# Turning values and keys by 64x64 products with the identity, head by head, in place of 128x128 transposes, in a two-layer hybrid decoder

## The chip, the cores and the metric

The kernel runs on one core of a Trainium2 chip. The time is the device time of one execution in microseconds (us), median of several runs. A profile of one execution gives each engine's instructions in order of time: TensorE (PE; its weight loads PEld), VectorE (DVE), ScalarE (ACT), GpSimd (POOL) and SyncE (SP).

## What is computed

Two layers, each of four sub-layers with a residual around each, on 512 tokens of width 1024 (batch 1), all in float32. The change lies in the second one, the mixer:

```python
h = h + 0.5 * swiglu_ffn(rmsnorm(h), ffn1_w_in, ffn1_w_out)
p = rmsnorm(h) @ w_mix_in                # conv | HGRN2 (6 heads of 64) | RWKV-7 (6 heads of 64)
y = concat(short_conv(p_conv), hgrn2(p_hg), rwkv7(p_rw))
h = h + y @ w_mix_out
h = h + memory_cross_attention(rmsnorm(h), rmsnorm(mem), wq, wkv, wo)
h = h + 0.5 * swiglu_ffn(rmsnorm(h), ffn2_w_in, ffn2_w_out)

# hgrn2, chunks of 64 tokens, a state of 64x64 for each head; b is the running sum of log_f in the chunk
o     = (qc * exp(b)) @ state + att @ vc
state = exp(b_last)[..., None] * state + (kc * exp(b_last - b)).T @ vc
# rwkv7, for each token
sa    = state @ a_t
state = state * w_t + outer(sa, b_t) + outer(v_t, k_t)
y_t   = state @ r_t
```

Both recurrences are done in the kernel by chunks of 64 tokens (8 chunks). A sum over the tokens of a chunk needs a factor with the tokens on the partitions. The projections leave channels on the partitions and tokens on the columns, so some tiles have to be turned, chunk by chunk and head by head: the RWKV values `v`, the HGRN values `v`, and the HGRN keys with their decay, `kh`.

## The kernel before, in words

All activations lie as tiles of 128 channels x 512 tokens (`s` in the profile; 2 heads of 64 channels in each). A projection (`mm3`, `group_steps`) multiplies a weight tile of 128x128 by such a tile three times in a rounded 32-bit format: rounded weight by rounded input, rounded weight by the input's rest, and the weight's rest by the rounded input. So each weight block of 128x1024 that SyncE loads into `wst` (2 buffers) is rounded by ScalarE into `whi` (3 buffers) and its rest is taken by VectorE into `wlo` (3 buffers) (`load_w`, lines 461 to 470). `split` (line 603) does the same with a result: ScalarE copies it rounded, VectorE subtracts. Results stand in PSUM: projections in `pb` (3 banks), small products in `pm` (3 banks, `small()`), the RWKV chain in `pt` (2 banks).

In the mixer (`mix`, line 1308) the projections are a queue (`Fill`): 28 of the input, then keys (`mem_kv`: four heads, two weights for each in one bank, 256 columns) and values (two matrices, each in two banks) of the memory for the cross-attention, then the first output projections `out(d, 5, 8)` with the HGRN part, and after everything else `out(d, 0, 5)`. Beside it stand generators: `rw_inputs` for three pairs of RWKV heads, `rw_solve`, `rw_chain` (8 steps, one for a chunk) and `rw_post` (the group norm: two rounds of sums over heads, a scale of the three tiles by ScalarE, low-rank products) one after the other, and `hg_pair` for three pairs of HGRN heads. Their products go between those of the queue. When is decided at build time: `Clock` estimates each instruction's time, a generator says with `Need(...)` which tiles, how many free buffers (`room`) and how many free `pm` banks (`banks=[(smalls, 2)]`) its next piece wants, and `Fill.run` (line 569) takes the piece that is ready by that estimate, or else one more projection product. TensorE's instructions stand in the order in which they were written so; those of ScalarE, VectorE and SyncE are sorted by the estimated start (`issue_in_order`, line 312). On the chip each engine keeps that order.

`turned` (line 794) is called nine times in a layer: three times by `rw_inputs`, into UV (tokens of one chunk and one head; the head `j` on the half of the partitions that `1 - j` names), and six times by `hg_pair` through `tok`, for `v` and `kh`. It makes eight transposes of 128 columns (both heads and two chunks in one) into two `pm` banks, one product of 64x64 for the first chunk of the head that the transposes, which start at each chunk, leave out, and takes out what is needed in five ScalarE copies. `half(j)` are 64 partitions, `cols(c)` the 64 columns of a chunk, `c8` splits the columns by chunks.

Of the kernel before, what the change touches and what calls it, by code (L numbers as in the profile page):

```python
# [18 lines left out]
P = 128  # L19
# [8 lines left out]
C = 64  # L28
H = C // 2
NC_ = T // C  # L30
# [299 lines left out]
def trunk(ctx: ExitStack, tc: tile.TileContext, a, out, parts=("ffn1", "mix", "xa", "ffn2"), dbg=None):  # L330
    nc = tc.nc
    clock = Clock()
    ve, se, gp = (Timed(clock, e, n) for e, n in ((nc.vector, "DVE"), (nc.scalar, "ACT"), (nc.gpsimd, "POOL")))
# [16 lines left out]
    te = Pe()  # L350
# [13 lines left out]
    smalls = Banks(clock, psml, [P, T], "pm", 3)  # L364
    serials = Banks(clock, pser, [P, T], "pt", 2)
    wst, whi, wlo = (Banks(clock, wpool, [P, 1024], n, k) for n, k in (("wst", 2), ("whi", 3), ("wlo", 3)))
    big, small, serial = bigs.get, smalls.get, serials.get
# [37 lines left out]
    ident = cst[:, C_ID:C_ID + P]  # L405
# [351 lines left out]
    def c8(x):  # L757
        return x.rearrange("p (c t) -> p c t", t=C)
# [32 lines left out]
            return x.rearrange("p (c n u t) -> p c n u t", c=NC_, u=2, t=hl)[:, :, :, 1, :]  # L791
        ve.copy_predicated(v(dst), m.bitcast(I32), v(src))

    def turned(x, low, dst):


        high = 1 - low
        hs = slice(high * C, high * C + C)
        for hf in range(2):
            ps = small()  # L800
            for w in range(4):
                c = 4 * hf + w
                if c < NC_ - 1:
                    te.transpose(ps[:, w * P:(w + 1) * P], x[:, c * C:c * C + P], ident)
                else:
                    te.transpose(ps[0:C, w * P:(w + 1) * P], x[:, c * C:], ident)
                    te.matmul(ps[C:P, w * P + high * C:w * P + high * C + C], x[hs, 0:C], ident[hs, hs],
                              start=True, stop=True)
            pv = ps.rearrange("p (c j e) -> p c j e", j=2, e=C)
            se.copy(dst(low, 4 * hf, 4 * hf + 4), pv[0:C, :, low, :])  # L810
            nw = 3 + (hf == 0)
            se.copy(dst(high, 4 * hf + 1, 4 * hf + 1 + nw), pv[C:P, 0:nw, high, :])
            if hf:
                se.copy(dst(high, 0, 1), pv[C:P, 3:4, high, :])

    def evac(n, ps):
        t = sl.get()
# [3 lines left out]
    def head_sum(src):  # L821
        ps = small()
        te.matmul(ps, blk, src, start=True, stop=True)
        return ps
# [10 lines left out]
    def rw_inputs(l, n, st, p):  # L835
        UV, Z, lr, X = st["UV"], st["Z"], st["lr"], st["X"]
# [5 lines left out]
        ps = small()  # L842
# [3 lines left out]
        ps = small()  # L846
# [18 lines left out]
        ps = head_sum(t0)  # L865
# [14 lines left out]
        for hf in range(2):  # L880
# [7 lines left out]
            e = c8(G[:, tt])  # L888
# [8 lines left out]
        sl.put(lw, ag, kk, G)  # L897
        yield Need(keys=[(l, f"v{p}")])
        v = X[f"v{p}"]
        yield Need(v, banks=[(smalls, 2)])  # L900

        turned(v, 1, lambda j, c0, c1: UV[C - j * C:P - j * C, c0:c1, 2 * p + j, :])
        yield Need(room=5, spare=False)
        MSa, MSr = [sl.get() for _ in range(2)], [sl.get() for _ in range(2)]
        for hf in range(2):
# [21 lines left out]
        for hf in range(2):  # L927
            bkh = BKH[hf]
            yield Need(bkh, banks=[(smalls, 1)])
            ps = small()  # L930
# [17 lines left out]
        ps = small()  # L948
        for c in range(NC_):
            for j in range(2):  # L950
                te.matmul(ps[half(j), cols(c)], MSa[j][half(1 - j), cols(c)], UV[half(1 - j), c, 2 * p + j, :],
                          start=True, stop=True)
        se.activation(Z[:, :, p, :], c8(ps), AF.Copy)
        ps = head_sum(t0)
# [6 lines left out]
    def half(j):  # L961
        return slice(j * C, j * C + C)

    def cols(c, w=C):
        return slice(c * w, (c + 1) * w)
# [220 lines left out]
    def hg_pair(l, st, p, ys):  # L1186
        yield Need(keys=[(l, f"hg{p}")], room=11 if p else 7)
        q, k, v, g, b, kh, dec = yield from hg_gates(l, st, p)


        def tok(x):
            y = sl.get()
            turned(x, 0, lambda j, c0, c1: c8(y)[j * C:j * C + C, c0:c1, :])
            return y

        yield Need(v, banks=[(smalls, 2)], room=4)
        vT = tok(v)
        sl.put(v)

# [39 lines left out]
        w = scaled(LEVELS[0])  # L1239
        yield Need(k, q, banks=[(smalls, 1)])  # L1240
        scores(k, q, 6)
        yield Need(kh, banks=[(smalls, 2)], room=2)
        khT = tok(kh)
        sl.put(kh)
        for i, hl in enumerate(LEVELS):
# [4 lines left out]
            w = w2  # L1250
            if i == 1:

                yield Need(khT, vT, banks=[(smalls, 1)], room=1)
                ps = small()
# [17 lines left out]
        ps = small()  # L1272
# [10 lines left out]
        ps = head_sum(t)  # L1283
# [418 lines left out]
```

## Time and profile before

| | |
|---|---|
| median of 3 runs | 2441.75 us (2440.54 to 2447.37) |
| the profiled execution | 2447.83 us, its span 2446.0 us |
| TensorE busy in the span | 2398.0 us (98%) |
| VectorE busy | 1389.6 us (57%) |
| ScalarE busy | 995.7 us (41%), 94.9 of it 74 table loads |

The span is cut out of the profiled execution; what lies around it is 1.8 us. Idle time of an engine is written in square brackets behind an instruction, with the instruction that ended it; in grouped rows it stands last. A table load is ScalarE's change of function tables, an instruction of its own (ACT_TABLE_LOAD). Unrounded products (all `pm` and `pt` products) are recorded twice each, transposes and rounded products once. In a row over several instructions the second number is the time from the start of the first to the end of the last; neighbours in a pipeline overlap.

### The profile page before, as it was taken

To read this page: it belongs to the slowest core of one execution; us is meant where nothing else is said; L and a number is where in the kernel's file an instruction comes from. 1 tells how busy PE (TensorE), PEld (TensorE's weight loads), DVE (VectorE), ACT (ScalarE), POOL (GpSimd) and SP (SyncE) were. 2 spreads that over 40 slices of the span, in tenths; PEclk is the share of its full clock that TensorE was granted. 3 is DMA by queue.
4 is the path that set the end of the run, shared out by engine and by line. 5 is a ranking of instruction groups with operands and counts; after the bars stand their busy time and mean duration, and the time that the engine had idled before them with its cause. 6 is when DMAs were issued, how large, how long until landed. Compare 5 with 4: busy or idle time off the path is not lost. (4 is left out here: it accounts for less than half of the span.)

```text
span 2446.0 us, 33922 instructions
## 1 busy us (share of the span) xinstructions
PE 2398.0 (98%) x13812; PEld 1971.5 (81%) x13812; DVE 1389.6 (57%) x2172; ACT 995.7 (41%) x1416; POOL 20.8 (1%) x22
## 2 busy tenths in 40 slices
PE   7999999999999999999999999999999999999997
PEld 6888887787878888888888888877887788888886
DVE  5444456798866654444544444567987756434444
ACT  4222235756654432222332222466475534323222
POOL 0000000000000000000000000000000000000000
PEclk9999999999999999999999999999999999999998
DMA  5333333243422233333323333423333313232332
GB/s 166 95 95 94 99 109 103 82 150 122 134 84 80 65 103 97 102 93 97 95 95 100 98 95 95 132 82 121 121 117 118 96 48 100 92 98 94 96 99 74
DMA packets 94315, 246.84 MB, mean 101 GB/s; under 512 B 22096, under 2 KB 24784, under 8 KB 94160
## 3 DMA queue, kind: packets, MB, share of 16 engines
q1 hardware_dynamic: 90848, 238.56, 31.6%
q10 hardware_dynamic: 3312, 6.12, 0.7%
q8 instruction: 109, 1.79, 0.3%
q14 instruction: 46, 0.38, 0.1%
HBM read 230.48 MB, written 14.16 MB: 100 GB/s over the span
## 5 line engine op out<-in xcount | busy, mean ns | idle before, releaser
L340 PE MATMUL pb<-s,whi 128*128 128x512 f32 (+1 forms) x6160 | 1897.6, 390 | 24.3 <-ACT whi L285 16.7
L340 PEld LDWEIGHTS pb<-s,whi 128*128 128x128 f32 x6160 | 1150.2, 189 | 268.1 <-ACT whi L285 20.6
L340 PE MATMUL pb<-s,wlo 128*128 128x512 f32 (+1 forms) x3080 | 1193.5, 388 | 5.6 <-DVE wlo L285 5.6
L285 ACT ACTIVATE whi<-wst 128x1024 fp32r<-128x1024 f32 (+5 forms) x445 | 434.2, 976 | 1033.9 <-PE pb L340 637.6
L340 PEld LDWEIGHTS pb<-s,wlo 128*128 128x128 f32 x3080 | 582.9, 189 | 123.9 <-DVE wlo L285 7.7
L285 DVE TENSOR_TENSOR wlo<-wst,whi 128x1024 fp32r<-128x1024 f32 (+5 forms) x445 | 498.4, 1121 | 134.8 <-ACT whi L285 127.1
L285 DVE TENSOR_TENSOR s<-pb,s 128x512 f32<-128x512 f32 (+1 forms) x345 | 236.0, 689 | 465.0 <-PE pb L340 443.4
L285 ACT ACTIVATE s<-s 128x512 f32<-128x512 f32 (+2 forms) x458 | 282.7, 626 | 246.8 <-DVE s L285 241.2
L285 DVE TENSOR_TENSOR s<-s,s 128x512 f32<-128x512 f32 (+3 forms) x526 | 317.0, 621 | 97.0 <-ACT s L285 92.1
L285 DVE SCALAR_TENSOR_TENSOR s<-pb,s 128x512 f32<-128x512 f32 x96 | 66.4, 692 | 234.5 <-PE pb L340 234.5
L285 ACT ACT_TABLE_LOAD x74 | 94.9, 1283 | 2.9 <-PEq L1690 1.7
L285 DVE SCALAR_TENSOR_TENSOR s<-s,vec,s 128x512 fp32r<-128x512 f32 (+2 forms) x100 | 74.3, 748 | 3.8 <-ACT s L285 2.9
L340 PEld LDWEIGHTS pm<-s,s 64*64 64x64 f32 (+2 forms) x1104 | 60.4, 158 | 10.0 <-issue 4.3
L340 PE MATMUL pm<-s,s 64*64 64x64 f32 (+2 forms) x1104 | 66.7, 248 | 1.7 <-DVE s L285 0.9
L285 ACT ACTIVATE s<-s,vec 128x512 fp32r<-128x512 f32 (+1 forms) x90 | 64.3, 718 | 3.3 <-DMA s<-xT 1.7
L340 PE MATMUL pb<-whi,s 128*128 128x512 f32 x128 | 49.5, 427 | 3.3 <-DVE s L285 3.3
L340 PEld LDWEIGHTS pm<-s 64*64 64x64 f32 (+1 forms) x1152 | 33.8, 132 | 4.7 <-issue 3.2
L340 PE MATMUL pm<-s 64*64 64x32 f32 (+1 forms) x1152 | 36.3, 216 | 0.0
L285 POOL TENSOR_TENSOR rms<-rms,mhalf 128x4 f32<-128x4 f32 (+1 forms) x10 | 17.1, 1714 | 2120.7 <-DVE rms L285 2120.7
L340 PEld LDWEIGHTS pb<-whi,s 128*128 128x128 f32 x128 | 24.1, 188 | 10.8 <-DVE s L285 4.1
L285 DVE TENSOR_TENSOR s<-s 128x256 f32<-128x256 f32 (+1 forms) x79 | 31.7, 439 | 0.2
L285 ACT ACTIVATE s<-pb 128x512 fp32r<-128x512 f32 x32 | 19.0, 594 | 29.5 <-PE pb L340 29.2
(106 smaller groups left out, 741.1 us busy)
## 6 DMA issues: line engine op xcount, KB each, us to landing
wst<-ffn_w_in SPq DMA_DIRECT2D x175, 512.0 KB, 3.4
wst<-w_mix_in SPq DMA_DIRECT2D x58, 512.0 KB, 3.6
wst<-ffn_w_out SPq DMA_DIRECT2D x64, 448.0 KB, 3.3
wst<-ffn_w_out SPq DMA_DIRECT2D x32, 512.0 KB, 3.5
wst<-xattn_wk SPq DMA_DIRECT2D x16, 512.0 KB, 4.4
wst<-xattn_wv SPq DMA_DIRECT2D x16, 512.0 KB, 3.7
wst<-xattn_wq SPq DMA_DIRECT2D x16, 512.0 KB, 3.5
wst<-xattn_wo SPq DMA_DIRECT2D x32, 256.0 KB, 2.6
```

Of the source, the lines that this page charges most:

```text
L285: ins = fn(*args, **kw)
L340: self.pin(nc.tensor.matmul(*args, **kw))
```

## The change

`turned` no longer transposes. It makes 16 products of 64x64, one for each chunk and head: the 64 channels of a head and the 64 tokens of a chunk are the stationary side, the matching 64x64 corner of the identity the moving one. All go into one `pm` bank, in the place where they are wanted, and the bank is returned. `tok` copies it out whole, `rw_inputs` in two halves of the partitions. The three places that asked for two free `pm` banks ask for one.

```diff
@@ -791,27 +791,14 @@
             return x.rearrange("p (c n u t) -> p c n u t", c=NC_, u=2, t=hl)[:, :, :, 1, :]
         ve.copy_predicated(v(dst), m.bitcast(I32), v(src))
 
-    def turned(x, low, dst):
-
-
-        high = 1 - low
-        hs = slice(high * C, high * C + C)
-        for hf in range(2):
-            ps = small()
-            for w in range(4):
-                c = 4 * hf + w
-                if c < NC_ - 1:
-                    te.transpose(ps[:, w * P:(w + 1) * P], x[:, c * C:c * C + P], ident)
-                else:
-                    te.transpose(ps[0:C, w * P:(w + 1) * P], x[:, c * C:], ident)
-                    te.matmul(ps[C:P, w * P + high * C:w * P + high * C + C], x[hs, 0:C], ident[hs, hs],
-                              start=True, stop=True)
-            pv = ps.rearrange("p (c j e) -> p c j e", j=2, e=C)
-            se.copy(dst(low, 4 * hf, 4 * hf + 4), pv[0:C, :, low, :])
-            nw = 3 + (hf == 0)
-            se.copy(dst(high, 4 * hf + 1, 4 * hf + 1 + nw), pv[C:P, 0:nw, high, :])
-            if hf:
-                se.copy(dst(high, 0, 1), pv[C:P, 3:4, high, :])
+    def turned(x, low):
+
+
+        ps = small()
+        for c in range(NC_):
+            for j in range(2):
+                te.matmul(ps[half(j ^ low), cols(c)], x[half(j), cols(c)], ident[half(j), half(j)], start=True, stop=True)
+        return ps
 
     def evac(n, ps):
         t = sl.get()
@@ -897,9 +884,11 @@
         sl.put(lw, ag, kk, G)
         yield Need(keys=[(l, f"v{p}")])
         v = X[f"v{p}"]
-        yield Need(v, banks=[(smalls, 2)])
-
-        turned(v, 1, lambda j, c0, c1: UV[C - j * C:P - j * C, c0:c1, 2 * p + j, :])
+        yield Need(v, banks=[(smalls, 1)])
+
+        ps = turned(v, 1)
+        for j in range(2):
+            se.copy(UV[half(1 - j), :, 2 * p + j, :], c8(ps)[half(1 - j)])
         yield Need(room=5, spare=False)
         MSa, MSr = [sl.get() for _ in range(2)], [sl.get() for _ in range(2)]
         for hf in range(2):
@@ -1190,10 +1179,10 @@
 
         def tok(x):
             y = sl.get()
-            turned(x, 0, lambda j, c0, c1: c8(y)[j * C:j * C + C, c0:c1, :])
+            se.copy(y, turned(x, 0))
             return y
 
-        yield Need(v, banks=[(smalls, 2)], room=4)
+        yield Need(v, banks=[(smalls, 1)], room=4)
         vT = tok(v)
         sl.put(v)
 
@@ -1239,7 +1228,7 @@
         w = scaled(LEVELS[0])
         yield Need(k, q, banks=[(smalls, 1)])
         scores(k, q, 6)
-        yield Need(kh, banks=[(smalls, 2)], room=2)
+        yield Need(kh, banks=[(smalls, 1)], room=2)
         khT = tok(kh)
         sl.put(kh)
         for i, hl in enumerate(LEVELS):
```

Because the planner sees other products, other copies and other needs, it writes the mixer in another order. Three places follow, each first as it stands before and then as it stands in the changed kernel. Names are out<-in, `s_309_4722` is one tile with its number.

**ScalarE, at the keys of head 1 in the first layer.** The last row of each piece is the rounding of the second weight of that head. Before:

```order
L285 ACT_TABLE_LOAD
L285 ACTIVATE s_309_4722<-s_309_4722 128x512
L285 ACTIVATE s_308_4721<-s_307_4720 128x512
L285 ACTIVATE s_306_4719<-s_306_4719 128x512
L285 ACT_TABLE_LOAD
L285 ACTIVATE s_309_4722<-s_309_4722 128x512
L285 ACTIVATE s_306_4719<-s_306_4719 128x512
L285 ACT_TABLE_LOAD
L285 ACTIVATE s_311_4763<-s_311_4763 128x512
L285 ACTIVATE s_311_4763<-s_311_4763,oml 128x512
L285 ACTIVATE whi<-wst 128x1024
```

After:

```order
L285 ACT_TABLE_LOAD
L285 ACTIVATE s_300_4703<-s_300_4703 128x512
L285 ACTIVATE s_300_4703<-s_300_4703,oml 128x512
L285 ACTIVATE s_301_4717<-s_297_4613 128x512
L285 ACT_TABLE_LOAD
L285 ACTIVATE s_299_4698<-pm,eps_c 128x512
L285 ACT_TABLE_LOAD
L285 ACTIVATE s_299_4698<-s_299_4698 128x512
L285 ACTIVATE s_313_4776<-s_313_4776 128x512
L285 ACTIVATE s_303_4743<-s_298_4696 128x512
L285 ACTIVATE s_312_4775<-s_311_4774 128x512
L285 ACTIVATE whi<-wst 128x1024
```

The rounding of the head's first weight stands 20 rows above the last row in the piece of before, and 13 above it in that of after; five table loads stand between the two before, three after.

**VectorE, at the first value matrix.** `s_351_5621<-pb` (before) and `s_357_5761<-pb` (after) are the rests of the first bank of the first value matrix, the row behind with `<-pb` that of its second bank; `s_...<-s_...` over 256 elements are HGRN score weights. Before:

```order
L285 TENSOR_TENSOR wlo<-wst,whi 128x1024
L285 COPY_PREDICATED s_333_5170<-cst,pm 128x32x8
L285 TENSOR_TENSOR s_349_5605<-s_322_4955 128x128x2 x2
L285 TENSOR_TENSOR s_351_5621<-pb,s_350_5620 128x512
L285 TENSOR_TENSOR s_349_5605<-s_321_4951,s_349_5605 128x128x2
L285 TENSOR_TENSOR s_349_5605<-s_302_4711,s_349_5605 128x128x2
L285 TENSOR_TENSOR wlo<-wst,whi 128x1024
L285 TENSOR_TENSOR s_353_5625<-pb,s_352_5624 128x512
L285 COPY UV<-pt 64x3x64
```

After:

```order
L285 TENSOR_TENSOR s_355_5715<-s_327_5042 128x256 x2
L285 COPY UV<-pt 64x3x64
L285 TENSOR_TENSOR s_355_5715<-s_321_4957,s_355_5715 128x256
L285 TENSOR_TENSOR s_355_5715<-s_306_4765,s_355_5715 128x256
L285 TENSOR_TENSOR wlo<-wst,whi 128x1024 x2
L285 TENSOR_TENSOR s_357_5761<-pb,s_356_5760 128x512
L285 TENSOR_TENSOR s_359_5765<-pb,s_358_5764 128x512
L285 COPY_PREDICATED s_338_5337<-cst,pm 128x128x2
L285 TENSOR_TENSOR s_360_5791<-s_306_4765,s_360_5791 128x512
L285 SCALAR_TENSOR_TENSOR rwS<-rwS,pc_2833,pt 128x64
```

The two rests stand next to each other now. From the rest of key head 1's second weight to the first of them there are 105 instructions of VectorE before (the former included, the latter not) and 122 after.

**ScalarE, at the end of the mixer.** The two rows `s_...<-pb` round the two banks of the second value matrix; rows with `gneps_c` belong to the group norm's variance, rows with `vec` to its scales, `whi` rows of 384 columns to the weights of `out(d, 5, 8)`. Before:

```order
L285 ACTIVATE s_375_5994<-pb 128x512
L285 ACTIVATE s_377_5998<-pb 128x512
L285 ACTIVATE whi<-wst 128x384
L285 ACTIVATE UV<-pt 64x3x64
L285 ACTIVATE whi<-wst 128x384
L285 ACTIVATE Z<-pt 128x192
L285 ACTIVATE whi<-wst 128x384
L285 ACTIVATE s_384_6057<-s_383_6053 128x512
L285 ACTIVATE s_386_6063<-s_385_6059 128x512
L285 ACTIVATE s_388_6069<-s_387_6065 128x512
L285 ACT_TABLE_LOAD
L285 ACTIVATE s_384_6057<-pm,gneps_c 128x512
```

After:

```order
L285 ACT_TABLE_LOAD
L285 ACTIVATE s_380_6025<-s_380_6025 128x512
L285 ACTIVATE s_382_6031<-s_382_6031 128x512
L285 ACTIVATE s_379_6021<-s_379_6021,vec 128x512
L285 ACTIVATE s_381_6027<-s_381_6027,vec 128x512
L285 ACTIVATE s_384_6037<-s_384_6037 128x512
L285 DMA lr<-lowrank 128x768
L285 ACTIVATE whi<-wst 128x384
L285 ACTIVATE s_383_6033<-s_383_6033,vec 128x512
L285 ACTIVATE s_385_6078<-pb 128x512
L285 ACTIVATE s_387_6082<-pb 128x512
L285 ACTIVATE whi<-wst 128x384
```

The two copies out of `pb` stand ahead of the group norm's rows before, and behind its third scale after.

## Rows read from the trace of the kernel before

**Rows 1.** The page, engines: busy time, share of the span, instructions.

```profile
PE 2398.0 (98%) x13812; PEld 1971.5 (81%) x13812; DVE 1389.6 (57%) x2172; ACT 995.7 (41%) x1416; POOL 20.8 (1%) x22
```

**Rows 2.** TensorE in order of time: start us, us, ... [idle before <-releaser].

```profile
604.80 0.51 PE L340 MATMUL pb<-s,whi 128*128 128x256 f32 x2 [3.34 <-ACT whi L285]
606.06 0.57 PE L340 MATMUL pb<-s,wlo 128*128 128x256 f32 x1 [0.75 <-DVE wlo L285]
606.43 1.91 PE L344 MATMUL pm<-cst,s 128*128 128x128 f32 x8
...
660.35 0.50 PE L340 MATMUL pb<-whi,s 128*128 128x512 f32 x1 [1.64 <-DVE s L285]
...
711.83 0.62 PE L340 MATMUL pb<-s,whi 128*128 128x512 f32 x2
712.29 0.39 PE L340 MATMUL pb<-s,wlo 128*128 128x512 f32 x1
714.86 0.78 PE L340 MATMUL pb<-s,whi 128*128 128x512 f32 x2 [2.18 <-DVE s L285]
...
1807.53 0.76 PE L340 MATMUL pb<-s,whi 128*128 128x256 f32 x2 [3.34 <-ACT whi L285]
```

**Rows 3.** TensorE in order of time, one call of `turned` and what follows.

```profile
422.52 1.03 PE L344 MATMUL pm<-cst,s 128*128 128x128 f32 x8
423.49 0.33 PE L340 MATMUL pm<-cst,s 64*64 64x64 f32 x2
423.74 0.73 PE L340 MATMUL pb<-s,whi 128*128 128x512 f32 x2
```

**Rows 4.** Windows: stretch, length, busy PE PEld DVE ACT POOL, PEclk, DMA, GB/s.

```profile
606.00:660.00 54.00, 52.65 (x785) 45.74 (x785) 47.19 (x106) 35.83 (x68) 0.00 (x0) 0.97 0.39 119
714.00:720.00 6.00, 5.14 (x16) 4.09 (x17) 3.47 (x6) 1.23 (x3) 0.00 (x0) 0.72 0.49 117
```

**Rows 5.** ScalarE's groups, 587 to 604 us: busy, mean ns | idle before.

```profile
L285 ACT ACT_TABLE_LOAD x5 | 6.4, 1283 | 0.1
L285 ACT ACTIVATE s<-s 128x512 f32<-128x512 f32 x10 | 5.9, 625 | 0.1
L285 ACT ACTIVATE whi<-wst 128x1024 fp32r<-128x1024 f32 x2 | 2.1, 1051 | 1.3 <-PE pb L340 1.3
L285 ACT ACTIVATE s<-s,oml 128x512 f32<-128x512 f32 x1 | 0.7, 722 | 0.0
```

**Rows 6.** TensorE in order of time: Z's 16 products, then a sum over heads.

```profile
440.43 1.15 PE L340 MATMUL pm<-UV,s 64*64 64x64 f32 x32
441.51 1.13 PE L340 MATMUL pm<-s,cst 128*128 128x512 f32 x2
442.07 1.02 PE L340 MATMUL pb<-s,whi 128*128 128x512 f32 x2
```

**Rows 7.** ScalarE's copies out of `pm`, whole span, grouped by shape.

```profile
L285 ACT COPY s<-pm 64x256 f32<-64x256 f32 x36 | 13.1, 363 | 3.9 <-PE pm L344 3.4
L285 ACT COPY s<-pm 128x512 f32<-128x512 f32 x9 | 5.3, 588 | 5.3 <-PE pm L340 5.3
```

**Rows 8.** VectorE in order of time: a weight's rest, a value bank's rest.

```profile
604.78 1.23 DVE L285 TENSOR_TENSOR wlo<-wst,whi 128x1024 fp32r<-128x1024 f32 x1 [0.76 <-ACT whi L285]
...
659.61 0.69 DVE L285 TENSOR_TENSOR s<-pb,s 128x512 fp32r<-128x512 f32 x1
```

**Rows 9.** VectorE's groups by shape, 604.7 to 660.4 us.

```profile
L285 DVE TENSOR_TENSOR s<-s,s 128x256 f32<-128x256 f32 x21 | 8.0, 421 | 1.7 <-ACT s L285 1.4
L285 DVE SCALAR_TENSOR_TENSOR s<-s,dec,pm 128x64 f32<-128x64 f32 x12 | 3.4, 279 | 0.3
```

**Rows 10.** TensorE in order of time: the group norm's first sums.

```profile
692.42 2.74 PE L340 MATMUL pm<-Z,cst 128*128 128x512 f32 x6
694.59 0.79 PE L340 MATMUL pb<-s,whi 128*128 128x512 f32 x1
```

**Rows 11.** ScalarE in order of time: the group norm's third scale.

```profile
705.29 0.82 ACT L285 ACTIVATE s<-s,vec 128x512 f32<-128x512 f32 x1 [0.43 <-DVE s L285]
```

## The prediction

> **What bounds the kernel now.** I read the page first, then stages, then waits. The page's first part has TensorE busy for 98% of the span [rows 1]; the time is therefore TensorE's own work plus the places where it stands still. The transposes that change lie only in the two mixer stages (about 395 to 716 us, and 1202.7 us later in the second layer), so I looked for TensorE's waits there, in order of time [rows 2]. Three in each layer are over a microsecond and come after the first `turned` (the same one stands at 604.80 and at 1807.53): at 604.80 it waits 3.34 us for ScalarE's rounding of a key weight and 0.75 us more for the low part; call it A, 4.1 us. At 660.35 it waits 1.64 us for VectorE (B). At 714.86 it waits 2.18 us for VectorE (C). What the reader is to see besides: after A and C the same instructions take longer. Eight transposes that take 1.03 us at full clock [rows 3] take 1.91 us at 606.43 [rows 2], and the granted clock from 714 to 720 is 0.72 [rows 4], so some products ran at 1.2 instead of 2.4 GHz, after a wait. 6 us at 0.72 is 1.7 us of lost work.
>
> The stage windows show who is behind it: from 606 to 660 VectorE is busy 47.2 of 54 us [rows 4], and between 587 and 604 ScalarE hardly rests: it is idle 1.3 us before the first weight's rounding, and 0.1 us or less before the groups of work that come between it and A [rows 5]. So in the middle of the mixer all three engines are near their limit, and what counts is the order in which the instructions stand.
>
> **The part that is certain: TensorE's own work.** One `turned` takes from 422.52 to 423.74: eight transposes 0.97 us, the pair of records of one 64x64 product 0.25 us, together 1.22 us [rows 3]. After the change it is 16 products of 64x64 from the two halves of the partitions into one bank. The trace has just that shape: Z's 16 products (32 records, since an unrounded product is recorded twice) take from 440.43 to 441.51, 1.08 us [rows 6]. 18 calls x (1.08 - 1.22) = -2.5 us in all, -1.3 us a layer. The bounds: 1.08 us is the same tile positions, so the gain could be a little more only if the return to rounded products is cheaper (0); if each product had to stand alone, as the single one does, 16 x 0.25 = 4.0 us.
>
> The Trainium skill, Perfetto Trace Analysis (Optimizing Tensor Performance, Transposes), says that logical transposes should use the transpose instruction and not a standard product, and TensorEngine Tiling (Array Packing), Gotcha 1, says that different row tiles cannot use one PSUM bank at the same time. Both speak against this change. By these rules the sum would be the 4.0 us per call and +50 us; row 6, two row halves into one bank at 0.07 us a product, does not bear them out, and I keep 1.08.
>
> **ScalarE's copies.** Before, a call has three copies of 64x256 at 0.363 us and two smaller ones (64x192 and 64x64) at less: 1.1 us and at most 0.7, I take 1.6. After, an HGRN call has one of 128x512 (0.588 us), an RWKV call two of 64x512, for which I take the same 0.588 each, since 256 elements take 0.363 on 64 partitions and the cost goes with elements [rows 7]. 12 x 1.02 + 6 x 0.43 = 14.8 us less. The order shows ScalarE with 70 table loads in place of 74, another 4 x 1.283 = 5.1 us [rows 5]. None of it is on TensorE's path by itself. The cover is TensorE's projection work; where the cover is gone, at A, B and C, the new order decides.
>
> **A.** What is late is the rounding of the second weight of key head 1. In the order of before, five table loads (6.4 us), ten activations (5.9) and one scaled by `oml` (0.7) stand between the roundings of the first and the second weight, 13.0 us [rows 5], and TensorE has eaten the first weight by then. Now there are three loads (3.85), eight activations at 0.625 and the scaled one 0.72: 9.6 us. The first rounding can't start before the last convolution projection ends (its buffer), and by the order stands behind a copy of an output that TensorE makes just before it: 0.6 us after that end. 0.6 + 1.04 + 9.6 + 1.04 = 12.3 us, and I add 0.6 for waits on VectorE (none before, but the rows alternate with it). TensorE has until then 72 products of 256 columns at 0.12 us (half of 0.23, which one of 512 takes: 711.83 to 712.29 for two) [rows 2], 18 small ones at 0.07, a sum over heads 0.55 (441.51 to 442.07) [rows 6], three returns to rounded products at 0.18 (0.25 - 0.07): 11.0 us. The wait is 1.9 + 0.75 = 2.7 us where it was 4.1: -1.4 us. Bounds: 0 and 6 (four more activations). Half speed follows in both.
>
> **B.** TensorE waits for VectorE to take the rest of the first value matrix out of its first bank: of the three `pb` banks the second value matrix needs that one for its second half. From the low part of the weight of A (604.78) to this subtraction (659.61), VectorE needed 54.8 us [rows 8]. In the new order 122 instructions stand there for 105, 17 more: one low part 1.23 and two of 512 elements at 0.69 [rows 8], seven of 256 at 0.42 and three of 64 at 0.28 [rows 9], and two copies, an add and a predicated copy at some 0.4: 1.2 + 1.4 + 2.9 + 0.8 + 1.6 = 7.9 us. TensorE has more there too: 98 more small products (2 levels of scores, 30 output products, one step of the chain and a half) at 0.07 = 6.6, one sum over heads 0.55, five returns 0.9, less 0.6 for four turns: 7.5 us. If VectorE rests between them as long as before, the wait becomes 1.6 + 7.9 - 7.5 = 2.0 us: +0.4. Queued behind it stand the next chain step and VectorE's state update. Bounds 0 and 6.
>
> **C.** Before, 54 products of the first output projection lie between the group norm's first sums (692.42 [rows 10]) and the second output projection (714.86); now 84, 12 of them the last value products. 30 x 0.23 = 6.9 us more cover, so the wait of 2.2 us goes. But the two value banks' copies on ScalarE now stand behind the group norm's third scale (its end, 705.29 + 0.82 [rows 11], is 13.7 us after 692.42), where they stood before all of it. The second output product needs the first of these banks. High 0.6 and low 0.69 end at 15.0; TensorE is there after 2.17 each for the two rounds of sums (692.42 to 694.59), 21 products 4.8, the three low-rank products 1.7 (as a sum over heads each) and four returns 0.7 = 11.6. It waits 3.4 us, and where VectorE's adds come late two products on perhaps another 0 to 1.2: I take 4.0 in all. The half speed after it falls into time that waits anyway (0.5) instead of 1.7 in front of full work. 4.5 against 3.9: +0.6, bounds -3.9 and +5.
>
> **Sum.** -1.3 (own work) -1.4 (A) +0.4 (B) +0.6 (C) and two more returns +0.4 is -1.3 us a layer; both layers have the same order in both kernels, so -2.6 us of the profiled 2447.8 us (span 2446.0). The median of the runs is 6 us lower; I take the difference from it: **2439 us**.
>
> **The rivals.** 1, faster: the copies of C are not late, because TensorE has lost enough in B to let ScalarE catch up, and A nearly closes, being under 1 us. Then 2 x (-1.3 - 3.3 + 0.4 - 3.3) is -15: 2427 us. For it speaks the longer cover after the norm; against it that ScalarE's copies stand in order behind the scales, which need TensorE's own sums first. 2, slower: VectorE is the bound from 606 to 660 and gets no less work. With A shorter and every gap of ScalarE's answered by a gap of VectorE's (it rests 54 - 47.2 = 6.8 us there [rows 4]), B grows to 6 us, and its own half-speed stretch (1.7) follows: 2 x (-1.3 - 1.4 + 4.4 + 1.7 + 0.6 + 0.4) is +9: 2451 us. It decides from a wait of about 5 us in B upwards. 3: the products stand alone, +50 us, 2492 us; the two pages named above state what would cause it. 4: the planner's new order gives all waits back as they were, and only the products count: -2.5 us, the same 2439 us by another way, so I count it into the forecast.
>
> **How the numbers follow.** A difference under 0.3%, 7.3 us, can hardly be told from none. Forecast with 4: 0.56, faster: 0.22, slower: 0.20, 3: 0.02. So faster 0.22, same 0.56, slower 0.22. The likeliest case's own range is 2432 to 2447. The range reaches from rival 1's time to a little past rival 2's, **2427 to 2453**; it leaves out rival 3 and cases in which A and C both vanish, or B and C both reach their bound.
>
> **What would show it.** In the changed profile: `turned` at about 1.08 us from its first product to the next instruction (4 us: rival 3). Copies out of `pm` of 0.59 us, and 70 table loads. The wait for ScalarE's rounding in key head 1 at 2 to 3 us, not 3.34; the wait for VectorE at the second value matrix near 2; no wait before the second output projection, but one of 3 to 4 us at the second product of the first one. If that last one is missing I am wrong on the fast side, by up to 9 us; if the wait at the value matrices is over 5 us, on the slow side.

## The result and the profile after

The change made the kernel slower: 2454.2 us (median of 6 runs, 2452.9 to 2458.6) against 2441.8 us (6 runs, 2439.4 to 2447.7), a ratio of 1.0049, 95% interval 1.0036 to 1.0062. The profiled execution has a span of 2452.3 us. The first profile of the kernel before, the one that the prediction read, was one of its slower executions; a second one, taken with the experiments below, has a span of 2441.2 us, TensorE busy for 2393.0 us of it, and the same waits, and is compared here where half speed matters. "Half speed" is a stretch in which the granted clock shows 1.2 GHz in place of 2.4.

What the change does by itself came as worked out. TensorE in order of time, one `turned` and the products behind it, against [rows 3]:

```profile
420.79 1.15 PE L340 MATMUL pm<-cst,s 64*64 64x64 f32 x32
421.87 1.16 PE L340 MATMUL pm<-s,s 64*128 64x128 f32 x16
```

1.08 us in place of 1.22. ScalarE's groups by shape, whole span (busy, mean ns | idle before), against [rows 7]:

```profile
L285 ACT ACT_TABLE_LOAD x70 | 89.8, 1283 | 2.9 <-PEq L1679 1.7
L285 ACT COPY s<-pm 128x512 f32<-128x512 f32 x21 | 12.3, 584 | 17.0 <-PE pm L340 16.9
L285 ACT COPY UV<-pm 64x512 f32<-64x512 f32 x12 | 7.0, 581 | 15.5 <-PE pm L340 15.4
```

The page's first part has 20.9 us less of ScalarE's work and 2 us less of TensorE's than [rows 1]:

```profile
PE 2396.0 (98%) x14208; PEld 1968.7 (80%) x14208; DVE 1390.9 (57%) x2172; ACT 974.8 (40%) x1346; POOL 20.8 (1%) x22
```

And still it takes longer, because TensorE stands still for longer in the mixer. The view of waits (us in total, times, longest), first layer's mixer (395 to 730 us) and second layer's (1590 to 1945 us), of the second profile of before:

```profile
PE pb L340 <- DVE s L285: 3.8, 2, 2.2
PE pb L340 <- ACT whi L285: 3.3, 1, 3.3
PE pb L340 <- DVE wlo L285: 2.0, 2, 1.3
...
PE pb L340 <- DVE s L285: 3.6, 2, 1.9
PE pb L340 <- ACT whi L285: 3.3, 1, 3.3
PE pb L340 <- DVE wlo L285: 1.7, 2, 1.3
```

The same view of the changed kernel:

```profile
PE pb L340 <- DVE s L285: 7.6, 3, 4.0
PE pb L340 <- ACT whi L285: 3.0, 1, 3.0
PE pb L340 <- DVE wlo L285: 1.8, 2, 1.3
...
PE pb L340 <- DVE s L285: 7.3, 3, 4.5
PE pb L340 <- ACT whi L285: 3.1, 1, 3.1
PE pb L340 <- DVE wlo L285: 2.1, 2, 1.3
```

The sums are 17.7 and 24.9 us: 7.2 us more, nearly all of it for VectorE's results. The view leaves out the smallest gaps: by the page, span less busy time, TensorE is idle for 56.3 us in place of 48.2 (48.0 in the first profile), 8.1 us more. TensorE in order of time shows where they stand, against [rows 2]:

```profile
602.42 0.80 PE L340 MATMUL pb<-s,whi 128*128 128x256 f32 x2 [2.99 <-ACT whi L285]
603.75 0.58 PE L340 MATMUL pb<-s,wlo 128*128 128x256 f32 x1 [0.54 <-DVE wlo L285]
...
669.68 0.50 PE L340 MATMUL pb<-whi,s 128*128 128x512 f32 x1 [4.04 <-DVE s L285]
...
705.59 0.73 PE L340 MATMUL pb<-s,whi 128*128 128x512 f32 x2 [3.03 <-DVE s L285]
...
712.53 0.70 PE L340 MATMUL pb<-s,whi 128*128 128x512 f32 x2 [0.52 <-DVE s L285]
...
1877.78 0.80 PE L340 MATMUL pb<-whi,s 128*128 128x512 f32 x1 [4.52 <-DVE s L285]
```

A is 3.5 us in the first layer and 4.0 in the second, B has gone from 1.6 to 4.0 and 4.5, and C has moved to the second output product, as worked out, with 3.0 us (2.5 in the second layer).

Half speed comes on top. In windows (length, busy PE PEld DVE ACT POOL, PEclk, DMA, GB/s) the granted clock behind B, 660 to 690 us, was 1.00 before; in the changed kernel it is 0.89, so 3.3 us of TensorE's work are lost there (the second profile of before, then the changed kernel):

```profile
660.00:690.00 30.00, 28.77 (x464) 22.77 (x465) 19.50 (x43) 19.49 (x32) 0.00 (x0) 1.00 0.41 126
660.00:690.00 30.00, 25.96 (x322) 20.08 (x321) 16.29 (x33) 14.22 (x23) 0.00 (x0) 0.89 0.24 80
```

Windows of 5 us from 30 to 2420 us, each with its length times what is missing from full clock, add up to 10.2 us in the second profile of before and 15.4 us in the changed kernel. But a stretch of half speed that lies in a wait costs nothing there. With TensorE's busy time in place of the length, in windows of 0.25 us over these stretches, the work lost is 9.3 and 13.2 us; below, "lost" is this figure. So the 11.1 us between these two spans are 8.1 us of idle time and 3.9 us of half speed, less 0.9 us of TensorE's own work. The last is what is left over: two profiles of the same kernel (before) differ by 0.8 us in it.

### The profile page after: what moved, and what is told of

Same layout as the page of the kernel before. It is cut to its first block, busy times and chain, and to the rows that moved or that the text cites. A ratio compares the mean times of both kernels' runs of the same rounds, so it can differ in the third digit from the quotient of the medians.

```text
span 2452.3 us, 34636 instructions
## 1 busy us (share of the span) xinstructions
PE 2396.0 (98%) x14208; PEld 1968.7 (80%) x14208; DVE 1390.9 (57%) x2172; ACT 974.8 (40%) x1346; POOL 20.8 (1%) x22
## 5 line engine op out<-in xcount | busy, mean ns | idle before, releaser
L340 PE MATMUL pm<-s,s 64*64 64x64 f32 (+2 forms) x1104 | 66.5, 247 | 1.7 <-DVE s L285 0.9
L340 PEld LDWEIGHTS pm<-cst,s 64*64 64x64 f32 (+1 forms) x652 | 30.0, 150 | 7.6 <-issue 3.5
L340 PE MATMUL pm<-cst,s 64*64 64x64 f32 (+1 forms) x652 | 31.6, 233 | 2.2 <-DVE s L285 2.2
```

What stands on the lines that cost most here:

```text
L340: self.pin(nc.tensor.matmul(*args, **kw))
```

## The experiments

Each was timed beside the kernel before on the same chip; a ratio is to those runs, with its 95% interval. In the diffs "-" is the kernel that is edited. Eighteen kernels were run.

### The old order with the new products, the new order with the old ones

First: `turned` of the kernel before, where the planner is told of the old transposes and copies, but the new ones are issued. VectorE's, SyncE's and GpSimd's order is that of before, word for word.

```diff
-                    te.transpose(ps[:, w * P:(w + 1) * P], x[:, c * C:c * C + P], ident)
+                    clock.note("PE", "transpose", (ps[:, w * P:(w + 1) * P], x[:, c * C:c * C + P], ident), {})
...
+            if hf:
+                for c in range(NC_):
+                    for j in range(2):
+                        te.pin(nc.tensor.matmul(ps[half(j ^ low), cols(c)], x[half(j), cols(c)], ident[half(j), half(j)],
```

> The order of before on every engine, with the new products (16 of 64x64 into one bank) and the new copies (one or two) standing where the old ones stood. Order theory (the added time comes from the new order of the mixer, above all from the wait at the second value matrix and the half speed after it): the turning itself gains 2.5 us and ScalarE some microseconds off the path, so 2437 to 2441 us. Turning theory (the products or the larger copies cost the time): as slow as the changed kernel, 2452 to 2456 us.

2444.1 us, 1.0014 (1.0005 to 1.0023): neither. The waits are those of before to 0.4 us (17.3 us by the same view; idle time 48.2 us, as before), TensorE's own work is 2.2 us less, and yet it is slower: in its profile half speed loses 12.6 us in place of 9.3. So the order theory holds for the waits, and the time is not explained by them alone. That is taken up in the last group.

Second: the same the other way round, with a second bank taken for the old transposes.

```diff
-                te.matmul(ps[half(j ^ low), cols(c)], x[half(j), cols(c)], ident[half(j), half(j)], start=True, stop=True)
+                clock.note("PE", "matmul", (ps[half(j ^ low), cols(c)], x[half(j), cols(c)], ident[half(j), half(j)]),
...
+                    te.pin(nc.tensor.transpose(pb[:, w * P:(w + 1) * P], x[:, c * C:c * C + P], ident))
```

> The order of the changed kernel on every engine, with the old transposes into two banks and the five old copies standing where the new ones stood. Order theory: as slow as the changed kernel or slower, by the 2.5 us of the transposes and something for the second bank and ScalarE's extra copies: 2455 to 2464 us. Turning theory: back to before, 2440 to 2446 us.

2466.0 us, 1.0101 (1.0087 to 1.0114): 12 us slower than the changed kernel. 2.6 us of that in each layer is a new wait at the first RWKV scores (426.4 us), which find the second bank taken. The turning theory, by which it would have come back to 2440 to 2446 us, is out: in the new order the old turning, with its second bank and its copies, is the worse one.

Third, the kernel before once more.

> The kernel before, unchanged, for a second profile and for the size of the noise: ratio 1.000 within 0.2%, runs between 2439 and 2448 us. If the spread of before is half-speed stretches that come and go, a profile near 2441 us shows fewer of them than the first one (which shows them after the waits at 604, 660, 714, 866, 1808, 1864, 1920 and 2071 us); if it is something else, the same stretches stand there and the time differs elsewhere.

2441.2 us, 1.000 (0.999 to 1.001), runs from 2438.7 to 2447.4. Its profile lacks the stretches of half speed at 866, 1864 and 2071 us; the waits are the same.

### What makes B wait

In the changed kernel a value weight's load stands in SyncE's order behind the group norm's fetches, and the wait runs on from engine to engine: SyncE issues the load at 659.70, ScalarE waits for it, an exponential stands behind that on ScalarE, VectorE waits for the exponential, and the subtraction of B (668.95) stands behind that on VectorE. SyncE, ScalarE and VectorE in order of time:

```profile
658.95 0.32 SPq L285 DMA_DIRECT2D s<-gd  x1
659.70 1.36 SPq L285 DMA_DIRECT2D wst<-xattn_wv  x1
...
664.39 1.06 ACT L285 ACTIVATE whi<-wst 128x1024 fp32r<-128x1024 f32 x1 [2.08 <-DMA wst<-xattn_wv]
665.35 0.61 ACT L285 ACTIVATE s<-s 128x512 f32<-128x512 f32 x1
...
666.00 0.76 DVE L285 TENSOR_TENSOR s<-s,s 128x256 f32<-128x256 f32 x2 [1.90 <-ACT s L285]
```

So the fetches were given to GpSimd's queue:

```diff
-        bon = [fetch(f"bon{p}") for p in range(3)]
-        gd = fetch("gd")
+        bon = [fetch(f"bon{p}", gp) for p in range(3)]
+        gd = fetch("gd", gp)
```

> The changed kernel, with the group norm's four fetches (three bonus tiles and gd) issued by GpSimd in place of SyncE; PE, DVE and ACT keep their order. Queue theory: the value weight's load no longer stands behind them on SyncE, ScalarE's wait for it (2.08 us) falls under 0.5, VectorE's wait behind it (1.90 us) too, TensorE's wait at the second value matrix falls from 4.0 to about 2, and with it perhaps the half speed: 2447 to 2451 us. Rival (VectorE has too much to do ahead of the subtraction, whenever the load lands): the wait stays near 4 us and the time at 2453 to 2455 us.

ScalarE's wait for the load is gone, VectorE's is 0.76 us, and B is 2.90 us in both layers: the queue was 1.1 to 1.6 us of it. But the time is 2455.2 us, 1.006 (1.0047 to 1.0073). Its profile, of the slowest of its five runs (2459.5 us), has 3.5 us less idle time than the changed kernel and 8.3 us more lost to half speed, 21.5 in place of 13.2; behind B these are 4.2 and 4.4 us in place of 3.4 and 2.1. How much of that a run at its median has was not seen.

The rest of B should be VectorE's load of work. Taking the key and value weights' rests from it:

```diff
-            ve.tensor_tensor(lo[:, cs], st[:, cs], f32(hi[:, cs]), op=ALU.subtract)
+            if src.name in ("xattn_wk", "xattn_wv"):
...
+                nc.gpsimd.tensor_tensor(lo[:, cs], st[:, cs], f32(hi[:, cs]), op=ALU.subtract)
```

> The changed kernel, with the rests of the cross-attention's key and value weights (16 subtractions of 1.22 us in each layer) made by GpSimd in place of VectorE; every other instruction keeps its place. Order theory in its present form (VectorE is the bound between the keys and the second value matrix, so that a wait taken away in one place comes back in another): with 14 us of VectorE's work gone there, the waits at the second value matrix and on the chain's state go for good, with the half speed behind them: 2438 to 2446 us, where GpSimd's slower subtraction adds some 1 to 3 us in each layer at key head 1. Rival (the wait comes from the memory transfers or from ScalarE's roundings): it stays at 3 to 4 us, 2452 us or above.

2463.2 us, 1.0091 (1.0078 to 1.0104), with B at 4.53 us. It doesn't decide: VectorE is held up while GpSimd subtracts. VectorE and GpSimd in order of time:

```profile
665.13 0.43 DVE L285 COPY_PREDICATED s<-cst,pm 128x256 f32<-128x256 int32 x1
665.46 2.39 DVE L285 TENSOR_TENSOR s<-s 128x256 f32<-128x256 f32 x1
```

```profile
665.18 2.38 POOL L473 TENSOR_TENSOR wlo<-wst,whi 128x1024 fp32r<-128x1024 f32 x1 [10.35 <-ACT whi L285]
```

A subtraction of 256 elements that takes 0.42 us elsewhere takes 2.39 us here. The same move in the kernel before:

> The kernel before with the same move to GpSimd: its wait of 1.64 us at the second value matrix goes, key head 1 gets 1 to 3 us later: 2438 to 2446 us. If the order was the cost of the change, this and the run before it come close together, or the changed one is ahead by the 2.5 us of the products; if the products or the copies have a cost of their own, the changed one stays 10 us behind.

2447.7 us, 1.0024 (1.0013 to 1.0035): also slower, with B at 1.45 us and TensorE waiting 2.2 us for the low part at A, and 15.5 us ahead of the run above. By the profiles 6.3 us of that are idle time (52.0 and 58.3) and 8.4 us half speed (10.5 and 18.9).

### Taking B away

The splits of the values are moved forward in ScalarE's and VectorE's order, by their planned time; nothing else moves.

```diff
+            mark = {e: len(q) for e, q in clock.queue.items()}
             vv.append([split(b) for b in box])
+            for e, q in clock.queue.items():
+                q[mark[e]:] = [(t - EARLY[free], i, ins) for t, i, ins in q[mark[e]:]]
```

First matrix, 4 us, in the changed kernel:

> The changed kernel, with the split of the first value matrix (two roundings on ScalarE, two subtractions on VectorE) four microseconds earlier in those two engines' orders, TensorE's order untouched. Order theory (the wait at the second value matrix, 4.0 and 4.5 us, and the half speed that follows it, 3.4 us of lost work in each layer, are most of the loss): the wait falls under 1 us, the half speed goes with it or shrinks, 2440 to 2447 us. Rival (all of this stage is VectorE's work, so the wait only moves to the next thing that VectorE owes): some other wait of 3 to 4 us stands behind it and the time stays at 2450 us or above.

2451.2 us, 1.0031 (1.0019 to 1.0043). B is gone, but 2.17 us of wait stand a few products further on, for the chain's state on VectorE:

```profile
671.82 0.91 PE L341 MATMUL pt<-rwS,s 64*64 64x64 f32 x12 [2.17 <-DVE rwS L285]
```

So the rival was right on the mechanism, at half its price. Second matrix too, 8 us:

> As the one before, and the split of the second value matrix too, eight microseconds earlier, ahead of the group norm's scales. Order theory: the wait after the low-rank products (3.0 and 2.5 us) goes as well, and a half-speed stretch of 1.7 us in one layer: 5 to 7 us less than the run before it, 2433 to 2441 us, under the kernel before. Rival: the group norm gets later by what the copies take, and its wait stands in front of the second output projection again: no gain over the run before it.

2450.5 us, 1.0024 (1.0014 to 1.0035): C is gone too, but its wait only moves, to another place than its rival had: 2.85 us stand a few output products later (709.07), for a bank whose sum VectorE adds behind the group norm's last steps. The first shift in the kernel before, and in the old order with the new products:

> The kernel before with the same shift of the first value matrix's split: its wait there (1.64 us in each layer) goes, and the half-speed stretch that follows it in some profiles. 2436 to 2440 us. If nothing is gained, a wait of 1.6 us there costs nothing that isn't paid elsewhere.

> The order of before with the new products and copies, and the same shift. It stands to the run before it as the new turning in the old order stands to the kernel before (3.6 us slower). If the products themselves gain 2.5 us and only half speed after that wait gives it back, it is now the faster of the two, 2434 to 2438 us; if the products bring a cost of their own wherever they stand, it stays 3 to 4 us above it.

2454.0 us, 1.0044 (1.0031 to 1.0056), and 2451.6 us, 1.0036 (1.0024 to 1.0047). Both got slower: instead of 1.6 us at B, the HGRN scores wait 2.5 us and three more places 0.4 to 0.6 each. VectorE can be given another order there, but not one that suits everybody. The new products are 2.4 us ahead of the old ones in this order (medians of runs that overlap).

### What moved the order, and A

The planner's needs alone:

```diff
-        yield Need(v, banks=[(smalls, 1)], room=4)
+        yield Need(v, banks=[(smalls, 2)], room=4)
```

(and at the two other places.)

> The changed kernel, with the planner's three needs set back to two free banks; products and copies stay as changed. It tells whether the needs or the costs (other products, fewer and other copies) moved the order. If the needs did, the order comes near that of before and the time near 2441 to 2445 us; if the costs did, the order stays near that of the changed kernel, with its wait of 3 to 5 us at the second value matrix, and the time at 2450 to 2458 us. The second is likelier, since the order of the build differs little from the changed kernel's.

2451.4 us, 1.0042 (1.0029 to 1.0055): the order stays near that of the changed kernel, as expected, though its waits at B are only 1.9 us. TensorE's idle time is 52.8 us, between the 48.2 of before and the 56.3 of the changed kernel. So the needs are a part of it, and the rest came with the costs that the planner adds up; which of them, of products or of copies, was not separated.

For A, the rounding of key head 1's second weight and its rest, 7 us earlier:

```diff
+            if src.name == "xattn_wk":
+                keys.append(1)
+                if len(keys) % 8 == 4:
+                    for q in clock.queue.values():
+                        q[-1] = (q[-1][0] - SOONER, *q[-1][1:])
```

> The order of before with the new products and copies, and the rounding of key head 1's second weight (ScalarE) and its rest (VectorE) seven microseconds earlier in their orders, ahead of two or three table loads. If the wait there (3.34 and 0.5 us in each layer) is that rounding's place alone, it goes, with the half speed behind it (3.4 us in each layer): 2444 - 7.6 - 6.8 is 2430 us, 2427 to 2438 us, under both kernels. If VectorE or the gates of the second HGRN pair then come late, a wait of 2 us or more stands at the pair's turned values instead and half of it is kept.

> The kernel before with the same move: 2441 - 7.9 - 3.4 to 5 is 2428 to 2430 us, 2426 to 2437 us. Beside the first of these four runs it shows what the products and copies are worth in one and the same order with fewer waits: 2.5 us for the new ones, or nothing, or a cost.

> The changed kernel with the same move: its wait at key head 1 (3.0 and 0.5, 3.2 and 0.8 us) and the half speed behind it (3.5 and 3.4 us) go, 2454 - 7.5 - 6.9 is 2440 us, 2437 to 2447 us; the waits at the second value matrix stay, 4 us, since nothing of them is touched, or grow where TensorE now comes to them earlier than VectorE does (then 2446 us or above).

The old order with the new products: 2439.1 us, 0.9989 (0.998 to 0.9999), the only one whose interval lies ahead of the kernel before. The kernel before: 2441.6 us, 0.9995 (0.9984 to 1.0006). The changed kernel: 2450.6 us, 1.0035 (1.002 to 1.005). The forecasts of 2428 to 2440 us all failed, because A only moves on: TensorE gets through the weight and then waits 3.85 us for a chain step's copy that stands behind the same table loads on ScalarE (old order with new products):

```profile
606.22 0.57 PE L341 MATMUL pt<-UV,s 128*64 128x64 f32 x12 [3.85 <-ACT UV L285]
```

In this order too the new products are 2.5 us ahead of the old ones, again by medians of runs that overlap.

### Half speed behind the same waits

The old order with the new products has the waits of before and was 3.6 us slower. Windows around A, of the second profile of before and of that run:

```profile
600.00:606.00 6.00, 2.66 (x22) 2.46 (x21) 5.20 (x10) 5.91 (x8) 0.00 (x0) 1.00 0.00 0
606.00:609.00 3.00, 2.24 (x12) 1.65 (x12) 2.72 (x4) 2.96 (x4) 0.00 (x0) 0.73 0.27 76
609.00:612.00 3.00, 3.00 (x19) 2.88 (x20) 1.99 (x3) 2.76 (x6) 0.00 (x0) 0.70 0.24 98
```

```profile
600.00:606.00 6.00, 2.61 (x27) 2.09 (x29) 5.14 (x8) 5.91 (x7) 0.00 (x0) 0.66 0.09 21
606.00:609.00 3.00, 3.00 (x26) 2.88 (x23) 1.99 (x3) 2.77 (x6) 0.00 (x0) 0.55 0.33 132
609.00:612.00 3.00, 3.00 (x65) 2.73 (x65) 1.52 (x3) 2.98 (x6) 0.00 (x0) 1.00 0.00 0
```

The wait is 3.34 us in both. In one the clock falls to 1.2 GHz after TensorE has gone on, and 1.7 us are lost. In the other it has fallen within the wait and stays low twice as long; 2.7 us are lost, since a part of the stretch passes while TensorE waits. TensorE in order of time, from the first product behind the wait to the next step of the chain, 6.57 us in the first and 6.93 in the second, where the new products are 0.14 us shorter and the wait for the low part is 0.46 us in place of 0.76:

```profile
605.71 0.50 PE L340 MATMUL pb<-s,whi 128*128 128x256 f32 x2 [3.34 <-ACT whi L285]
612.28 0.57 PE L340 MATMUL pt<-UV,s 128*64 128x64 f32 x12
```

```profile
602.93 0.80 PE L340 MATMUL pb<-s,whi 128*128 128x256 f32 x2 [3.34 <-ACT whi L285]
609.86 0.57 PE L340 MATMUL pt<-UV,s 128*64 128x64 f32 x12
```

To see whether the place alone does this, eight products, 1.8 us of work, were repeated in the first sub-layer, long before the mixer:

```diff
+        if len(groups) == 30:
+            for _ in range(8):
+                te.pin(nc.tensor.matmul(ps, w[0][:, :P], xs[0][0], start=True, stop=True))
```

> The order of before with the new products and copies (2444.1 us), and eight more products of 512 columns (1.8 us of TensorE's work, overwritten by what follows) in the first sub-layer, long before the mixer. If the 3.6 us by which it is slower than the kernel before is a matter of where the same waits fall against the stretches of half speed, the time moves by something else than 1.8 us: by 3.4 us less or more. If it is a cost of the products or copies, it is 2445.9 us within 0.7.

> The kernel before, with eight more products of 512 columns (1.8 us) in the first sub-layer, as in the shifted run of the old order with the new products. If the kernel before owes some of its lead to where its waits fall against the stretches of half speed, its runs now spread, 2440 to 2451 us, with a median of 2444 us or above; if it doesn't, they lie at 2442 to 2445 us with a few at 2449 us.

> The changed kernel with the same eight products more in the first sub-layer. The shifted kernel before is at 2448.6 us. If the waits (7.2 us more in the changed kernel, 1.4 us less of its own work) are what the order costs and the rest of the 12.5 us was the place of the half speed, the shifted pair stands nearer together: 2452 to 2457 us. If the order costs the whole 12.5 us whatever the place, 2459 to 2463 us.

> The kernel before with four more products (0.9 us) in the same place. If its 2441 us is a good place among the stretches of half speed, another shift gives 2443 to 2449 us too; if the one shift was an exception, 2441 to 2442.5 us.

The old order with the new products, shifted: 2444.2 us, runs from 2440.1 to 2451.3. The kernel before, shifted by eight: 2448.6 us (2444.4 to 2453.4), ratio 1.0023 (1.0012 to 1.0034); by four: 2446.9 us (2440.3 to 2449.2). The changed kernel, shifted: 2456.3 us (2455.1 to 2458.1). The waits are the same as without the shift within 1 us. So 1.8 us of work made the kernel before 8 us slower and the changed one 2 us, and the two stand 7.7 us apart in place of 12.5. They were timed on two chips; against the kernel before on its own chip each is 8.1 and 14.0 us slower, which is 5.9 us apart. In this pair of profiles TensorE is idle for 47.4 and 56.7 us, the waits of the two mixers being 17.3 and 25.9 us, and loses 16.4 and 13.7 us to half speed.

That the place does it is not shown. In the first layer the wait at A ends at 604.80 and 605.71 us in the two profiles of before, and at 604.59 in the shifted one: a stretch of half speed at about 43 us, which both of the former have and the latter hasn't, takes back 1.7 us of the shift. So the profiles do not put the waits 1.8 us later, and yet the shifted one lost 16.4 us, where the two had lost 15.1 and 9.3.

## Why the prediction was wrong

**Own work: right for one call.** It takes 1.08 us as forecast. -2.5 us were forecast for all of the products; two pairs with the same order and the same waits give -2.4 and -2.5 us (medians; their intervals overlap), the shifted pair, on two chips, -4.4, and the unshifted pair alone is the other way, +3.6. In each pair half speed differs by 1.6 to 3.9 us, so the times do not show the 2.5 by themselves. Rival 3, products that stand alone, didn't come. Of the two pages of the Trainium skill that the prediction named, only the one on row tiles and banks would set the products apart; here 16 products from two row halves into one bank take less than the transposes.

**A: the mechanism, not the size.** 3.5 and 4.0 us against 2.7, so that 0.6 us were gained in the first layer and none in the second (4.0 after 3.8), in place of 1.4. The prediction put 0.6 us for waits on VectorE between the two roundings; these were 0.24, but ScalarE also stands 2.10 us for a fetched HGRN tile (`hf`, at 591.71) before the gates, which had no term. Its reading of the kernel before, 13.0 us of work and no rest between the roundings, leaves out three pieces of 0.6, 0.6 and 0.3 us and a wait of 1.1 us ahead of the last of them (589.25); the sum for A does not use it.

**B: the step that failed.** "If VectorE rests between them as long as before." VectorE's work between the two points was sized well, 55.1 us after 48.0 (7.1 more, 7.9 forecast). But it rested 11.4 us in place of 6.8, as these two windows from the low part of A's weight to the subtraction of B show, of before and of the changed kernel:

```profile
604.78:659.61 54.83, 53.16 (x787) 46.03 (x787) 48.02 (x105) 36.74 (x67) 0.00 (x0) 0.97 0.38 116
```

```profile
602.48:668.95 66.47, 62.63 (x1073) 53.92 (x1073) 55.08 (x124) 40.58 (x64) 0.00 (x0) 0.95 0.41 129
```

What VectorE waits for most in these windows, before and after:

```profile
DVE s L285 <- ACT s L285: 2.3, 3, 1.2
DVE s L285 <- PE pm L340: 2.0, 1, 2.0
```

```profile
DVE s L285 <- PE pm L340: 4.8, 3, 2.2
DVE s L285 <- ACT s L285: 4.1, 5, 1.9
```

Of the 4.6 us, 1.8 are ScalarE's results: the wait of 1.9 us in the chain from SyncE's queue, and taking that away took 1.1 us from B (shown). The other 2.8 are TensorE's small products in `pm`; one of these waits, 1.99 us at 609.22, stands right behind A, where TensorE ran at half speed. So VectorE, which TensorE waits for at B, had itself waited for TensorE. 1.6 + (66.5 - 54.8) - 7.5 is 5.8 us; but TensorE's own busy time between the points grew by 9.5 us and not by 7.5 (62.63 after 53.16), of which 1.2 are more half speed behind A, and with it the sum is 3.8, against 4.0 measured. I looked at the orders of ScalarE and VectorE and not at SyncE's, and the section on the kernel says wrongly that SyncE's instructions are sorted by the planner's estimate: only ScalarE's and VectorE's are, and SyncE's follow from the build.

**C: right in the place, smaller in size.** 3.0 us at the place forecast, with 0.5 us more (2.5 and 0.3 in the second layer), against 3.4 to 4.0.

**Half speed: the other term that failed.** The forecast let it follow A as before, put 0.5 us for it behind C and left it out behind B. Behind B 3.4 and 2.1 us of work were lost in the two layers, where the second profile of before has none; behind A 2.9 and 3.1 in place of 1.7 and 2.5; behind C 0 and 1.7 in place of 1.7 twice. That is rival 2's mechanism, a larger B with its own half speed, which was given 0.20 and 2451 us. Its price for B (6 us) was too high and its half speed (1.7 us) too low. B stayed below the 5 us that were named as the sign of the slow case, and the kernel was slow all the same.

**The base.** The first profile of before had half speed behind B in the second layer and in two other places that the second profile doesn't have. I took the difference from the median and kept this profile's half speed in the terms. What the new order adds in idle time is steady: 8.3 us against the first profile of before, 8.1 against the second, 9.3 in the shifted pair. What half speed takes is not: 1.9 us less, 3.9 more and 2.7 less. So some 8 to 9 of the 12.5 us are waits of the new order, and how the rest divides into half speed and the gain of the products is open. The changed kernel was run at one shift only.

What stays open: what places the start of a half-speed stretch, which no run here separates from the length of the wait, and which of the planner's choices first brought more of VectorE's work ahead of B.

## What to carry to other kernels

In a stage where three engines are near their limit, a cheaper piece of work is worth its own time only if the order around it holds: build the new instructions into the old order, and the old ones into the new, and compare the idle time of the engine that bounds the kernel, which here told the two apart where the times did not. When a dense engine is waited for, a wait taken away in one place may come back a few products later, as it did here four times, so look at the total of the waits and not at the one that went. Count half speed only where the engine works: what falls into a wait is paid already. And when the differences are of the size of a few stretches of half speed, time each kernel at two or three shifts before ranking them.

## What the runs showed of the hardware

The granted clock fell within the same wait of 3.34 us or behind it, for 2.7 or 1.7 us of lost work, and 1.8 us more of work far ahead of it moved the median of an otherwise equal kernel by 8 us. The Trainium skill, TensorE: Matmul & The Clock Gate (Part 1, What's actually happening), says that how many products run slow varies from run to run of one kernel; the spread of the shifted runs, 2440 to 2451 us, agrees. It puts the cost of the clock's ramp at under 1% of a kernel's span; the 9.3 to 16.4 us lost in the profiles of the kernel before and its shifted form are 0.4 to 0.7%, which agrees, and the change measured here is 0.5%.

VectorE's subtraction of two SBUF operands took 2.39 us in place of 0.42 while GpSimd subtracted. The Trainium skill, Perfetto Trace Analysis (Optimizing Scalar/DVE Operations), warns that moving work between the two may not help because they share a port; the run agrees: it was 9 us slower than the changed kernel, by the profiles 2.0 us of idle time and 5.7 us of half speed among them.
